# Queries and keys projected with tokens in the array and normed per token; GLA level scores for four heads at once

## The chip, the cores and the metric

The program runs on one core of one Trainium2 chip. A core has five engines that run at the same time, each with its own instruction queue in program order: TensorE (PE, the matrix array; PEld is its loading of the stationary operand), VectorE (DVE), ScalarE (ACT), GpSimd (POOL) and SyncE (SP, which here issues weight transfers). The metric is device time in microseconds (us), from one execution's start to its end; the median of three runs is used.

## The reference

The model is two blocks. The first has two layers, each over 256 tokens x and 256 context tokens z of width 1024: half a SwiGLU feed-forward, token mixing, half a SwiGLU. The second block (fox attention and retention) is not touched. The token mixing projects the normed tokens with `w_in` and mixes with four methods side by side:

```python
na_q = lambda p: rms_norm(heads(p['na_q'], 4, 64), na_q_norm)      # na_k, gqa_q, gqa_k likewise
b_x = neighborhood_attention(na_q(px), na_k(px), na_v(px), kz_na, vz_na, na_rpb)
c_x = gla_output(ox_gla, px['gla_r'], gla_norm)                    # gated linear attention, 4 heads of 32
qx_gqa = apply_rope(gqa_q(px), cos, sin)                           # rotated by position, x only
kx_gqa = apply_rope(gqa_k(px), cos, sin)
d_x = block_attention(qx_gqa, concat([kx_gqa, kz_gqa]), concat([gqa_v(px), vz_gqa]))
out_x = concat([a_x, b_x, c_x, d_x])                               # a_x: a Fourier mix
```

`rms_norm` here runs over the 64 channels of one head of one token: `x * rsqrt(mean(x*x) + eps) * gain`. In the last layer only x goes on, so z needs keys and values there but no queries. GLA's decayed scores are computed at several levels (block sizes 64, 128, 32, 16, ... of the token axis), and the results are merged under masks.

## The kernel before

All data are fp32. Big matmuls keep fp32 precision by splitting both operands in a rounded part `hi` and a rest `lo` and doing three matmuls (`mm3`, L615 to L619: hi*hi, H_lo*hi, H_hi*lo). Activations live transposed: `H` holds channels on the partitions and tokens along the free axis (x in columns 0 to 255, XR; z in 256 to 511, ZR). Weights stream in chunks of 512 KB through SP's queue; ACT makes `hi` (L593), DVE makes `lo` (L595); `take` and `drop` hand a chunk's pair to its user and free it. `make_plan` lists the chunks in the order in which they are used.

The order of instructions on every engine is made in Python by a list scheduler (`Sched`, L327 to L411): each piece of work is a generator that yields an engine and an estimated time, and the piece that can start earliest is put next. A piece that fills only part of the array (`pe_part`: the level scores and the attention scores) is spaced out by a factor 1.7 among the others. On the chip each engine then runs its list in order.

`mix1` (L1179) does the token mixing. Its main thread goes through the windows of `w_in`: a window is one projection of some 128 columns over all tokens, 8 steps of `mm3`. The values (GV) are projected with tokens as the stationary operand, so that they come out with tokens on the partitions; queries and keys (NQ, NK, QQ, QK) are projected with the weights as the stationary operand, so that they come out transposed: 64 channels of a head on partitions and tokens along the free axis. In that form the mean over a head's channels runs across partitions: `normed` (L1519) copies the projection out, squares it on ACT (L1526), and `head_rstd` (L658) sums squares by tiny matmuls (L664, two columns per token tile), takes the power on POOL (L641), spreads the result by a copy (L669) and transposes it back (L673); DVE multiplies it in (L1530). For GQA's x tokens a rotation follows: a matmul with a permutation (L1536), DVE times sin (L1539), POOL times cos (L1542), POOL add (L1544).

Beside the windows run: `level` (L1306), which makes the decayed q and k of one GLA level (POOL differences L1321, ACT exp, DVE product) and lets `score` (L1378) multiply two heads at once, in two groups of 32 rows of the array (L1389), twice per level; `merge` brings them under the masks. `pair` (L1554) does two heads of attention: `scores` (L1601), `soft` (L1605: DVE maximum L655 or L1611, ACT exp L1617, DVE reciprocal L1621, DVE scale L1623, PE transposes L1627), and the product with the values (L1573). Neighbourhood attention adds a bias of 128 KB per head, loaded through POOL's queue (L1591) into two tiles. After the windows follow Fourier, GLA's outputs, what is left of attention, and then `w_out`.

At the start of `mix1` the second token range's norm is still in work: POOL's queue holds the load of the small parameters `pp` (L1192), memsets, two bias loads, two gains (L1200) and then the power `r` (L641) of that norm, which PE transposes (L649) and DVE multiplies in (L843, L848) to finish `H`.

Of the kernel before, what the change touches and what calls it, by code (L numbers as in the profile page):

```python
# [38 lines left out]
                          np.arange(C_QV, C_QV + 128)]).reshape(2, 336)  # L39
WOUT_ROWS = np.concatenate([np.arange(768), 768 + QPERM])  # L40
# [31 lines left out]
def rot_matrix(half, n):  # L72
    p = np.zeros((2 * half, 2 * half))
    for i in range(half):
        p[i, i + half] = -1.0
        p[i + half, i] = 1.0
    return block_diag(p, n).T


def consts1():  # L80
# [6 lines left out]
    c.add("ropeP", rot_matrix(32, 2))  # L87
# [4 lines left out]
    ang = ang.astype(np.float64)[:, p % 32].T  # L92
    c.add("cos", np.cos(ang))
    c.add("sin", np.sin(ang))
# [53 lines left out]
def params1(inp):  # L148
    packs = []
    for l in range(DEPTH):  # L150
# [8 lines left out]
        c.add("wg", wg)  # L159
        packs.append(c)  # L160
# [3 lines left out]
def params2(inp):  # L164
    packs = []
    for l in range(DEPTH):
# [10 lines left out]
             bgf=(5, 6), bgb=(6, 7), wg=(7, 263))  # L177
# [52 lines left out]
def make_plan():  # L230
# [19 lines left out]

    for l in range(DEPTH):
        ffn(("ffn1_w1", "ffn1_w3", "ffn1_w2"), l)
        last = l == DEPTH - 1
        if last:
            w("w_in", l, 0, KD, cols(C_GQ))
            for t in range(2):
                w("w_in", l, 0, KD, cols(C_NQ, t))
        for half in range(2):
            for k0, n in ((0, 3), (3, 3), (6, 2)):
                w("w_in", l, k0, n, GV_COLS[half])  # L260
# [4 lines left out]
        for t in range(2):  # L265
            w("w_in", l, 0, KD, cols(C_NK, t))
            if not last:
                w("w_in", l, 0, KD, cols(C_NQ, t))
        w("w_in", l, 0, KD, cols(C_QK))
        for t in range(2):  # L270
            w("w_in", l, 0, KD, C_QQ + QPERM[128 * t:128 * t + 128])
# [159 lines left out]
def pet(k=1):  # L431
    return "PE", k * 0.06
# [22 lines left out]
class Net:  # L455
# [723 lines left out]
    def mix1(self, l, last, hwait):  # L1179
# [8 lines left out]
        p_sem, lev_sem, pair_sem = Sem(nP), Sem(2), Sem(nPT // 2)  # L1188
        ev = defaultdict(Ev)

        pp = mp.tile([128, 263], F32, name="pp")
# [114 lines left out]
        def level(s):  # L1306
# [42 lines left out]
            left = [2]  # L1349
            for h in (0, 2):  # L1350
                self.spawn(score(s, h, Q, K, left))
# [26 lines left out]
        def score(s, h0, Q, K, left):  # L1378

            bs = []  # L1380
            for h in range(2):
                b = yield from self.bank()
                bs.append(b[:, :T])
            yield pe_part(128, 4 * ns)
            for u in range(2 * ns):
                i = u ^ 1 if s == 128 else u
                for h in range(2):
                    r = 32 * (h0 + h)
                    PE.matmul(bs[h][:, 128 * u:128 * u + 128], K[r:r + 32, 128 * u:128 * u + 128],  # L1389
                              Q[r:r + 32, 128 * i:128 * i + 128], start=True, stop=True, tile_position=(r, 0))  # L1390
            left[0] -= 1
            if left[0] == 0:
                self.release(lev_sem)
            for h in range(2):
                self.spawn(merge(s, h0 + h, bs[h]))
# [832 lines left out]
```

## Time and profile before

| | before |
|---|---|
| median of 3 runs | 2482.75 us (2481.01 to 2484.56) |
| profiled execution | 2481.66 us, span 2479.9 us |
| mean granted TensorE clock | 0.996 |
| instructions | 38754 |
| busy PE / DVE / ACT / POOL | 98% / 64% / 39% / 20% of the span |

Busy shares are over the whole span; the token mixing of layer 0 lies at about 405 to 600 us and that of layer 1 at about 1400 to 1580 us. The times of the rows further down are counted from the span's start. A fp32 matmul shows as two records, hence twice the number of matmuls in the counts of L1389, L664 and L1536.

### The profile page before, as it was taken

To read this page: it belongs to the slowest core of one execution; us is meant where nothing else is said; L and a number is where in the kernel's file an instruction comes from. 1 tells how busy PE (TensorE), PEld (TensorE's weight loads), DVE (VectorE), ACT (ScalarE), POOL (GpSimd) and SP (SyncE) were. 2 spreads that over 40 slices of the span, in tenths; PEclk is the share of its full clock that TensorE was granted. 3 is DMA by queue.
4 is the path that set the end of the run, shared out by engine and by line. 5 is a ranking of instruction groups with operands and counts; after the bars stand their busy time and mean duration, and the time that the engine had idled before them with its cause. 6 is when DMAs were issued, how large, how long until landed. Compare 5 with 4: busy or idle time off the path is not lost.

```text
span 2479.9 us, 38754 instructions
## 1 busy us (share of the span) xinstructions
PE 2431.0 (98%) x15186; PEld 2120.1 (85%) x15186; DVE 1582.1 (64%) x2655; ACT 960.9 (39%) x1599; POOL 490.7 (20%) x492
## 2 busy tenths in 40 slices
PE   7999999999999999999999999999999999999998
PEld 5888888786888888888888887999988999988998
DVE  4878746566667676656652657766668655768654
ACT  4322224445432222332222345644535534445443
POOL 0201011331110101110101224100232422222322
PEclk9999999999999999999999999999999999999999
DMA  7665532210345553345642322555433654434652
GB/s 284 228 194 190 180 101 92 71 56 22 128 153 169 169 170 121 134 145 189 211 160 79 100 89 70 196 182 181 159 124 108 214 172 164 147 116 162 204 182 83
DMA packets 105735, 365.87 MB, mean 148 GB/s; under 512 B 13168, under 2 KB 15376, under 8 KB 105040
## 3 DMA queue, kind: packets, MB, share of 16 engines
q1 hardware_dynamic: 82768, 286.58, 35.1%
q10 hardware_dynamic: 21712, 72.98, 9.2%
q0 software_dynamic: 1072, 3.82, 0.5%
q8 instruction: 120, 1.97, 0.3%
q14 instruction: 63, 0.52, 0.1%
HBM read 360.09 MB, written 1.05 MB: 146 GB/s over the span
## 4 chain that ended last, share of the span: by engine, by line
PE 89%; DVE 4%; issue 3%; POOL 2%; ACT 1%; DMA 1%; POOLq 0%; DVEq 0%; SPq 0%; ACTq 0%
PE bank L617 27%; PE bank L618 27%; PE bank L619 27%; DVE lo L595 1%; PE bank L1573 1%; PE bank L1601 1%; POOL lev L1321 1%; DMA raw<-in_dram 1%; PE bank L1627 1%; POOL r L641 1%; ACT hi L593 1%; PE bank L1389 1%; PE bank L2027 0%; PE bank L2072 0%; PE bank L2008 0%
## 5 line engine op out<-in xcount | busy, mean ns | idle before, releaser
L617 PE MATMUL bank<-H_hi,hi 128*128 128x512 f32 (+3 forms) x3000 | 998.9, 334 | 0.3 <-ACT H_hi L846 0.3
L618 PE MATMUL bank<-H_lo,hi 128*128 128x512 f32 (+3 forms) x3000 | 984.5, 329 | 1.9 <-DVE H_lo L848 1.9
L619 PE MATMUL bank<-H_hi,lo 128*128 128x512 f32 (+3 forms) x3000 | 983.0, 328 | 2.1 <-DVE lo L595 2.1
L593 ACT CAST hi<-raw 128x1024 fp32r<-128x1024 f32 (+3 forms) x538 | 543.5, 1023 | 1017.6 <-PE bank L618 901.0
L595 DVE TENSOR_TENSOR lo<-raw,hi 128x1024 fp32r<-128x1024 f32 (+3 forms) x538 | 657.5, 1232 | 353.7 <-ACT hi L593 349.5
L617 PEld LDWEIGHTS bank<-H_hi,hi 128*128 128x128 f32 x3000 | 566.0, 189 | 60.5 <-issue 7.5
L619 PEld LDWEIGHTS bank<-H_hi,lo 128*128 128x128 f32 x3000 | 567.1, 189 | 53.2 <-DVE lo L595 2.5
L618 PEld LDWEIGHTS bank<-H_lo,hi 128*128 128x128 f32 x3000 | 567.6, 189 | 51.1 <-DVE H_lo L848 2.5
L617 PE MATMUL bank<-gh,hi 128*128 128x512 f32 (+2 forms) x1119 | 369.4, 330 | 1.1 <-ACT gh L925 1.1
L618 PE MATMUL bank<-gl,hi 128*128 128x512 f32 (+2 forms) x1119 | 369.0, 330 | 0.6 <-POOL gl L927 0.6
L619 PE MATMUL bank<-gh,lo 128*128 128x512 f32 (+2 forms) x1119 | 368.8, 330 | 0.0
L927 POOL TENSOR_TENSOR gl<-f,gh 128x512 fp32r<-128x512 f32 (+2 forms) x136 | 170.2, 1252 | 969.5 <-ACT gh L925 962.9
L720 DVE CUSTOM_DVE_ANT_0 prod<-mraw,crow 128x1024 f32<-128x1024 f32 x224 | 307.3, 1372 | 2.9
L617 PEld LDWEIGHTS bank<-gh,hi 128*128 128x128 f32 x1119 | 211.0, 189 | 22.5 <-ACT gh L925 1.5
L618 PEld LDWEIGHTS bank<-gl,hi 128*128 128x128 f32 x1119 | 211.1, 189 | 22.1 <-POOL gl L927 1.2
L619 PEld LDWEIGHTS bank<-gh,lo 128*128 128x128 f32 x1119 | 211.0, 189 | 20.7
L1025 DVE SCALAR_TENSOR_TENSOR X<-bank,mod,X 128x256 f32<-128x256 f32 x192 | 87.0, 480 | 137.2 <-PE bank L619 137.1
L925 ACT CAST gh<-f 128x512 fp32r<-128x512 f32 (+2 forms) x136 | 68.6, 506 | 141.0 <-DVE f L917 108.5
L910 POOL TENSOR_TENSOR s<-s,rstd 128x272 f32<-128x272 f32 (+1 forms) x44 | 66.9, 1521 | 184.8 <-ACT s L908 184.7
L641 POOL TENSOR_TENSOR r<-v,half 128x2 f32<-128x2 f32 (+3 forms) x43 | 48.1, 1120 | 193.1 <-DVE v L637 192.8
L917 DVE TENSOR_TENSOR f<-s,bank 128x512 f32<-128x512 f32 (+2 forms) x114 | 64.2, 564 | 34.5 <-POOL s L910 28.6
L804 POOL TENSOR_TENSOR acc<-acc,sq 128x256 f32<-128x256 f32 (+1 forms) x33 | 42.2, 1278 | 170.7 <-ACT sq L801 170.7
(279 smaller groups left out, 2017.1 us busy)
## 6 DMA issues: line engine op xcount, KB each, us to landing
raw<-in_dram SPq DMA_DIRECT2D x422, 512.0 KB, 3.4
mraw<-in_dram ACTq DMA_DIRECT2D x128, 512.0 KB, 4.3
raw<-in_dram SPq DMA_DIRECT2D x96, 448.0 KB, 3.3
mraw<-in_dram SPq DMA_DIRECT2D x16, 512.0 KB, 4.1
raw<-in_dram SPq DMA_DIRECT2D x8, 504.0 KB, 3.2
crow<-in_dram ACTq DMA_DIRECT2D x3, 1024.0 KB, 5.2
raw<-in_dram SPq DMA_DIRECT2D x8, 384.0 KB, 4.9
X<-in_dram SPq DMA_DIRECT2D x4, 512.0 KB, 8.1
```

What stands on the lines that cost most here:

```text
L593: self.ACT.copy(hi, raw)
L595: self.DVE.tensor_tensor(lo, raw, hi.bitcast(F32), op=ALU.subtract)
L617: self.PE.matmul(ps, a[0], b[0], start=first, stop=False)
L618: self.PE.matmul(ps, a[0], b[1], start=False, stop=False)
L619: self.PE.matmul(ps, a[1], b[0], start=False, stop=last)
L641: self.POOL.tensor_tensor(r[:, :n], v[:, :n], self.half[:, :n], op=ALU.pow)
L720: i = self.DVE.tensor_tensor_reduce(prod, got[c], rows[:, s], 1.0, 0.0, ALU.mult, ALU.add, m[:, s, k:k + 1])
L910: self.POOL.tensor_tensor(s, s, late[1], op=ALU.mult)
L917: self.DVE.tensor_tensor(f, s, pb[:, :w], op=ALU.mult)
L925: self.ACT.copy(hi, f)
L927: self.POOL.tensor_tensor(lo, f, hi.bitcast(F32), op=ALU.subtract)
L1025: self.DVE.scalar_tensor_tensor(o, ps[:, r[0] - r0:r[1] - r0], self.mods[l][i][:, s, m:m + 1], o, ALU.mult, ALU.add)
```

## The change

Normed queries and keys are projected like the values: tokens stationary, 256 or 384 columns (NK and QK in one) streaming, in passes of two token tiles (z tiles 2 and 3 first, then 0 and 1). They come out with tokens on the partitions, so that a head's mean runs along the free axis: ACT squares, DVE reduces per head and scales, POOL takes the power, DVE multiplies from the bank. GQA's x tokens are rotated by four DVE operations with tables that POOL makes at the start of `mix1` from cos, sin and the gains. Then PE transposes 128 x 128 blocks, and ACT copies them out with the gain. A pair of attention now waits for all token tiles of its queries and keys. `score` takes four banks and multiplies four heads in four groups of 32 rows; it is no longer spaced out as partial work.

```diff
-        def score(s, h0, Q, K, left):
+        def score(s, Q, K):
+            yield four_sem
             bs = []
-            for h in range(2):
+            for h in range(4):
                 b = yield from self.bank()
                 bs.append(b[:, :T])
-            yield pe_part(128, 4 * ns)
+            self.release(four_sem)
+            yield *pe32(128, 2 * ns), Sched.LAT
             for u in range(2 * ns):
                 i = u ^ 1 if s == 128 else u
-                for h in range(2):
-                    r = 32 * (h0 + h)
+                for h in range(4):
+                    r = 32 * h
                     PE.matmul(bs[h][:, 128 * u:128 * u + 128], K[r:r + 32, 128 * u:128 * u + 128],
                               Q[r:r + 32, 128 * i:128 * i + 128], start=True, stop=True, tile_position=(r, 0))
...
+        rope = mp.tile([128, 2, 2, 2, 64], F32, name="rope")
+        rows = mp.tile([128, 2, 64], F32, name="rows")
+        g = par("gqa_rows").rearrange("p (i c) -> p i c", i=2)
+        POOL.tensor_scalar(rows[:, 0], g[:, 0], 0.125, None, ALU.mult)
+        POOL.tensor_copy(rows[:, 1], g[:, 1])
+        for i in range(2):
+            for tt in range(2):
+                cs, sn = (self.c1(x)[:, 64 * tt:64 * tt + 64] for x in ("cos", "sin"))
+                POOL.tensor_tensor(rope[:, i, 0, tt], cs, rows[:, i], op=ALU.mult)
+                for a, b in ((0, 32), (32, 0)):
+                    POOL.tensor_tensor(rope[:, i, 1, tt, a:a + 32], sn[:, a:a + 32], rows[:, i, b:b + 32], op=ALU.mult)
+        def normed(tt, ps, parts):
...
+            ACT.activation(y, ps, AF.Square)
...
+            DVE.tensor_reduce(v, split(y), AX.X, ALU.add)
+            DVE.tensor_scalar(v, v, 1 / 64, EPS, ALU.mult, ALU.add)
...
+            POOL.tensor_tensor(rr, v, self.half[:, :nh], op=ALU.pow)
+            DVE.tensor_tensor(split(y), split(ps), rr.unsqueeze(2).to_broadcast([128, nh, 64]), op=ALU.mult)
...
+            for name, c, w, gain, i in parts:
+                if i is None or tt >= 2:
+                    continue
...
+            for j in range(0, n, 128):
+                PE.transpose(tp[:, j:j + 128], y[:, j:j + 128], self.ident)
...
-            rb = yield from self.head_rstd(sq, n)
...
-                PE.matmul(b[:, :256], self.c1("ropeP"), dst[:, :256], start=True, stop=True)
...
+            yield from self.wait_all([ev[q, 2 * s], ev[q, 2 * s + 1]] + [ev[k, t] for t in keys]
+                                     + [ev["v", h, t] for h in range(2) for t in keys])
...
+            yield from heads("nq", [(0, 1)])
...
+        yield from heads("k", [(2, 3), (0, 1)])
+        if not last:
+            yield from heads("nq", [(2, 3), (0, 1)])
```

Line numbers after the change are one lower up to `score` and higher behind it: L1389 is L1388, L641 is L640, L1601 is L1636, L1627 is L1662.

On POOL at the head of layer 1's mixing, before (a name left of the arrow is written, right of it read; `r` is the rstd of the second token range):

```order
103 L1591 DMA bias_10501<-in_dram 128x256
104 L1200 TENSOR_SCALAR gain_10478<-pp 128x1 x2
105 L641 TENSOR_TENSOR r<-v,half 128x2
106 L641 TENSOR_TENSOR r<-v,half 128x4 x2
107 L1321 TENSOR_TENSOR lev<-Fc 128x2x64 x2
```

and after:

```order
111 L1199 TENSOR_SCALAR gain_10635<-pp 128x1 x2
112 L1519 TENSOR_SCALAR rows<-pp 128x64
113 L1520 COPY rows<-pp 128x64
114 L1524 TENSOR_TENSOR rope<-k_mix,rows 128x64
115 L1526 TENSOR_TENSOR rope<-k_mix,rows 128x32 x2
116 L1524 TENSOR_TENSOR rope<-k_mix,rows 128x64
117 L1526 TENSOR_TENSOR rope<-k_mix,rows 128x32 x2
118 L1524 TENSOR_TENSOR rope<-k_mix,rows 128x64
119 L1526 TENSOR_TENSOR rope<-k_mix,rows 128x32 x2
120 L1524 TENSOR_TENSOR rope<-k_mix,rows 128x64
121 L1526 TENSOR_TENSOR rope<-k_mix,rows 128x32 x2
122 L640 TENSOR_TENSOR r<-v,half 128x2
```

Fourteen operations (`rows`, `rope`) now stand between the gains and `r`; the same rows stand at the head of layer 0.

On PE in layer 1's windows, before (L1389 the level scores, L664 and L673 the sums and the transposes of `head_rstd`, L1601 scores of neighbourhood attention, the rest projection):

```order
6461 L1389 MATMUL bank<-lev 128x128 x4
6462 L664 MATMUL bank<-k_mix,p_10484 128x2 x4
6463 L617 MATMUL bank<-H_hi,hi_64 128x512
6464 L618 MATMUL bank<-H_lo,hi_64 128x512
6465 L619 MATMUL bank<-H_hi,lo_65 128x512
6466 L1389 MATMUL bank<-lev 128x128 x4
6467 L617 MATMUL bank<-H_hi,hi_64 128x512
6468 L618 MATMUL bank<-H_lo,hi_64 128x512
6469 L619 MATMUL bank<-H_hi,lo_65 128x512
6470 L1601 MATMUL bank<-nk_10505,nq_10506 128x512 x2
6471 L673 MATMUL bank<-k_89,p_10484 128x128 x4
6472 L617 MATMUL bank<-H_hi,hi_64 128x512
```

and after (L1388 the level scores of four heads, the rest the projection with tokens in the array):

```order
6557 L618 MATMUL bank<-hi_68,H_lo 128x384
6558 L1388 MATMUL bank<-lev 128x128 x8
6559 L616 MATMUL bank<-hi_68,H_hi 128x384
6560 L617 MATMUL bank<-lo_69,H_hi 128x384
6561 L618 MATMUL bank<-hi_68,H_lo 128x384
6562 L1388 MATMUL bank<-lev 128x128 x8
6563 L616 MATMUL bank<-hi_70,H_hi 128x384
```

Groups of four matmuls have become groups of eight, and there are half as many; the sums (L664) are gone.

On PE at the end of layer 1's last window, after (L1636 the scores, L1568 the transposes of normed queries, L1662 the transposes of the softmax):

```order
6766 L617 MATMUL bank<-H_lo,hi_64 128x256
6767 L618 MATMUL bank<-H_hi,lo_65 128x256
6768 L1636 MATMUL bank<-nk,nq 128x512 x2
6769 L1568 MATMUL bank<-k_89,p_10640 128x128 x2
6770 L1434 MATMUL bank<-k_89,lev 128x128 x4
6771 L1568 MATMUL bank<-k_89,p_10641 128x128 x2
6772 L1444 MATMUL bank<-vt_10650,p_10640 128x256
6773 L1444 MATMUL bank<-vt_10651,p_10640 128x256
6774 L1662 MATMUL bank<-k_89,p_10639 128x128 x4
```

The scores of nk and nq, of which one stands among the projections in the PE rows of before (L1601), now begin behind the last projection.

## Rows read from the trace of the kernel before

**Rows 1.** Busy share of each engine, from the page

```profile
PE 2431.0 (98%) x15186; PEld 2120.1 (85%) x15186; DVE 1582.1 (64%) x2655; ACT 960.9 (39%) x1599; POOL 490.7 (20%) x492
```

**Rows 2.** Windows: from:to, length, busy us of each engine, clock, DMA

```profile
455.90:561.00 105.10, 101.94 (x627) 80.73 (x626) 66.11 (x112) 42.33 (x75) 40.20 (x47) 0.97 0.22 71
...
1530.00:1580.00 50.00, 48.11 (x373) 40.40 (x372) 34.87 (x72) 30.66 (x65) 11.58 (x12) 1.00 0.37 126
```

**Rows 3.** Timeline of PE, layer 0: start, us, line, records

```profile
461.09 0.39 PE L618 MATMUL bank<-H_lo,hi 128*128 128x512 f32 x1
...
461.32 0.39 PE L619 MATMUL bank<-H_hi,lo 128*128 128x512 f32 x1
...
461.64 1.16 PE L1389 MATMUL bank<-lev 32*128 32x128 f32 x16
...
463.07 0.40 PE L618 MATMUL bank<-H_lo,hi 128*128 128x512 f32 x1
```

**Rows 4.** Timeline of PE, layer 1, the same place

```profile
1478.75 0.40 PE L619 MATMUL bank<-H_hi,lo 128*128 128x512 f32 x1
...
1479.08 0.71 PE L1389 MATMUL bank<-lev 32*128 32x128 f32 x8
...
1480.06 0.40 PE L618 MATMUL bank<-H_lo,hi 128*128 128x512 f32 x1
```

**Rows 5.** PE's instructions by line and shape: records, busy us, mean ns

```profile
L664 PE MATMUL bank<-k_mix,p 128*128 128x2 f32 x108 | 13.8, 248 | 0.4 <-ACT p L1526 0.4
...
L1536 PE MATMUL bank<-qq,k_mix 128*128 128x256 f32 x8 | 2.4, 378 | 0.0
```

**Rows 6.** Timeline of PE at a group of L664, layer 0

```profile
465.40 1.05 PE L664 MATMUL bank<-k_mix,p 128*128 128x2 f32 x8
...
466.31 0.48 PE L617 MATMUL bank<-H_hi,hi 128*128 128x512 f32 x1
```

**Rows 7.** Timeline of PE, a projection of 256 columns

```profile
398.02 0.28 PE L619 MATMUL bank<-gh,lo 128*128 128x256 f32 x1
...
398.14 0.28 PE L617 MATMUL bank<-gh,hi 128*128 128x256 f32 x1
```

**Rows 8.** PE's waits in 408 to 640; timeline; window 480 to 500

```profile
PE bank L1627 <- DVE p L1623: 2.8, 4, 1.1
...
PE bank L673 <- DVE p L669: 0.8, 1, 0.8
...
498.10 0.63 PE L618 MATMUL bank<-H_lo,hi 128*128 128x512 f32 x1
...
498.53 0.63 PE L619 MATMUL bank<-H_hi,lo 128*128 128x512 f32 x1
...
480.00:500.00 20.00, 17.07 (x108) 11.64 (x110) 15.48 (x33) 8.44 (x16) 8.16 (x12) 0.91 0.17 53
```

**Rows 9.** Timeline of POOL, heads of layer 0 and layer 1

```profile
412.64 0.42 POOL L1200 TENSOR_SCALAR gain<-pp 128x1 f32<-128x1 f32 x2 [1.45 <-DMA pp<-in_dram]
...
413.04 0.97 POOL L641 TENSOR_TENSOR r<-v,half 128x2 f32<-128x2 f32 x1
...
1407.09 1.25 POOL L1200 TENSOR_SCALAR gain<-pp 128x1 f32<-128x1 f32 x2 [0.74 <-DMA pp<-in_dram]
...
1409.32 1.00 POOL L641 TENSOR_TENSOR r<-v,half 128x2 f32<-128x2 f32 x1 [0.98 <-DVE v L637]
```

**Rows 10.** DVE by line in 1500 to 1640; timeline of PE; POOL's line; DMA issues

```profile
L655 DVE CUSTOM_DVE_ANT_0 bank<-bank,bias 128x512 f32<-128x512 f32 x2 | 1.4, 696 | 0.0
...
L1623 DVE TENSOR_SCALAR p<-p,rs 128x512 f32<-128x512 f32 x6 | 3.1, 512 | 0.1
...
492.02 1.13 PE L1601 MATMUL bank<-nk,nq 64*128 64x512 f32 x4
...
L1591 POOL DMA_DIRECT2D bias<-in_dram x16 | 9.0, 566 | 19.1 <-DVE m L655 15.1 <-DVE m L656 3.4 <-DVE rs L1621 0.4
...
bias<-in_dram POOLq DMA_DIRECT2D x8, 128.0 KB, 2.5
```

More of the change, by code (lines that the diff above doesn't have):

```diff
@@ L91, in consts1 @@
                           (t % 64).astype(np.float32)[:, None] * inv], axis=1).astype(np.float32)
-    ang = ang.astype(np.float64)[:, p % 32].T
+    ang = ang.astype(np.float64)[:, np.arange(64) % 32].reshape(2, 128, 64).transpose(1, 0, 2)
     c.add("cos", np.cos(ang))
-    c.add("sin", np.sin(ang))
+    c.add("sin", np.where(np.arange(64) < 32, -1, 1) * np.sin(ang))
     a64 = 2 * np.pi * np.outer(np.arange(64), np.arange(64)) / 64
@@ L159, in params1 @@
         c.add("wg", wg)
+        c.add("gqa_rows", np.broadcast_to(np.concatenate([np.asarray(inp[n][l]) for n in ("gqa_q_norm", "gqa_k_norm")]),
+                                          (128, 128)))
         packs.append(c)
@@ L249, in ffn, with tok @@
                 w(names[2], l, k0, k1 - k0, cols(0, m))
+    def tok(l, name):
+        c, n = TOK[name]
+        for k in range(0, KD, n):
+            w("w_in", l, k, min(n, KD - k), c)
     for l in range(DEPTH):
@@ L255, in make_plan @@
             w("w_in", l, 0, KD, cols(C_GQ))
-            for t in range(2):
-                w("w_in", l, 0, KD, cols(C_NQ, t))
+            tok(l, "nq")
         for half in range(2):
-            for k0, n in ((0, 3), (3, 3), (6, 2)):
-                w("w_in", l, k0, n, GV_COLS[half])
+            tok(l, half)
             if half == 0:
@@ L264, in make_plan @@
                     w("w_in", l, 0, KD, cols(C_GQ))
[L265 to L271, printed above, removed]
+        tok(l, "k")
+        if not last:
+            tok(l, "nq")
+        tok(l, "qq")
         for t in range(2):
@@ L1348, in level @@
                 return
-            left = [2]
-            for h in (0, 2):
-                self.spawn(score(s, h, Q, K, left))
+            self.spawn(score(s, Q, K))
         def few(s, prods):
@@ L1552, in mix1, with pair @@
             POOL.memset(t[:, 256:], 0.0)
-        def pair(kt, s, q, k, keys, vcol, bias):
-            yield from self.wait_all([ev[q], ev[k]] + [ev["v", h, t] for h in range(2) for t in keys])
+        def pair(kt, s, q, qi, k, ki, keys, vcol, bias):
+            yield from self.wait_all([ev[q, 2 * s], ev[q, 2 * s + 1]] + [ev[k, t] for t in keys]
+                                     + [ev["v", h, t] for h in range(2) for t in keys])
             yield pair_sem
@@ L1564, in pair @@
                 sub += evs
-                self.spawn(scores(s, qn[q], qn[k], keys, qt, pT, bias, evs))
+                self.spawn(scores(s, qn[q][:, qi], qn[k][:, ki], keys, qt, pT, bias, evs))
             yield from self.wait_all(sub + [win_done])
@@ new lines, in mix1, with heads @@
+        NORMED = {"k": (("nk", 0, 256, par("na_k_norm"), None), ("qk", 256, 128, par("gqa_k_norm"), 1)),
+                  "nq": (("nq", 0, 256, gain8[:, 0:1], None),), "qq": (("qq", 0, 256, gain8[:, 1:2], 0),)}
+        def heads(name, passes):
+            yield from tok(name, passes, lambda t, ps: normed(t, ps, NORMED[name]))
+        if last:
+            w = yield from self.take("w_in", l, 0, KD, cols(C_GQ))
+            b = yield from self.bank()
+            yield from self.gemm([(b[:, :256], w)], self.H, *XR, lambda k: hwait(k, *XR))
+            self.drop()
+            gla_q(b[:, :256])
+            yield from heads("nq", [(0, 1)])
```

161 lines of the change are left out of this document (76 added, 85 removed).

## The prediction

> **What bounds the kernel now.** I read the page's busy shares first: TensorE (PE) is busy 98% of the span, VectorE (DVE) 64% [rows 1]. So a change pays by the PE time it removes, and costs where it makes PE wait. The windows by stage then show where that holds. The mixing stage of layer 0 has PE busy 101.94 of 105.10 us and DVE 66.11; before layer 1's w_out (1530 to 1580) PE has 48.11 of 50 and DVE 34.87 [rows 2]. The list of PE's instructions by line gives the sizes of what is removed, the timelines what each group costs between its neighbours, the waits what PE waits for. The sum is made against the profiled execution, 2481.66 us; the median of the runs is 1.09 us above it, and I add that at the end.
>
> **Level scores: fewer groups on PE.** A level's scores stand as a small group between projection matmuls. In layer 0 one group (8 matmuls, 16 records) pushes the next matmuls apart: from 461.32 to 463.07 there are 1.75 us, of which two steps of the projection's cadence (461.09 to 461.32, 0.23) are work that stands there anyway: 1.28 us per group [rows 3]. In layer 1 (half as many matmuls) it is 1480.06 - 1478.75 - 0.47 = 0.84 us [rows 4]. The four more matmuls cost 1.16 - 0.71 = 0.45 us [rows 3, 4], so 0.4 us of each group is entry and exit. After the change six groups of twice the matmuls stand in each layer where there were twelve. If four heads run at once, a new group lasts as long as an old one: 6 x 1.28 + 6 x 0.84 = 12.7 us saved. If only two run at once, as now, just twelve entries go: 12 x 0.4 = 4.8 us. I take 12.7, because the two heads of a group already run beside each other, and keep 4.8 as the end of the range. The Trainium skill, "TensorEngine Tiling (Array Packing)", Key Properties, says that different tiles of the array can load and multiply in parallel, which would give the 12.7, and that a change of tiling mode drains the engine, which agrees with the 0.4 us.
>
> **The rest that PE loses and gains.** The tiny matmuls of L664 (sums of squares per head): from the buffers `p` 108 records, 54 matmuls, 13.8 us busy [rows 5]; 48 of them, those of queries and keys, go: 12.3 us busy. In place, 1.05 us busy push the next matmul by 0.91 [rows 6], so 12.3 x 0.87 = 10.6 us. The rotation matmul L1536 lasts 0.6 us (two records of 378 ns [rows 5] that overlap a little); six go, 6 x 0.6 x 0.87 = 3.1 us. Transposes stay 28 and 20 in number, but in 20 groups instead of 14: at half a group's entry each, 6 x 0.2 = 1.2 us more. Projections: with tokens in the array, a matmul streams 256 or 384 columns instead of 512; 256 columns stand 0.12 apart [rows 7], two of them as long as one of 512, and 384 lies between, so the total changes by 0.4 us at most; I put +0.4. PE's own work: -12.7 - 10.6 - 3.1 + 1.2 + 0.4 = -24.8 us.
>
> **Waits in the windows of layer 0.** Now PE waits there four times, 2.8 us, on L1623 (the softmax scale) before the transposes L1627, and twice 0.8 us on the copy L669 before L673 [rows 8]. After two of these waits the 512-column matmuls stand 0.43 apart (498.10 to 498.53) instead of 0.23 [rows 8]: the granted clock of that stretch is 0.91 [rows 8], so its lower level (1.2 GHz) for about eight matmuls, 1.6 us. The order shows the neighbourhood softmaxes (nk, nq) behind the windows afterwards and L669 gone: -2.8 - 1.6 - 1.6 = -6.0. The new chain ACT square, DVE reduce, POOL power, DVE scale, PE transpose has a whole projection pass as cover; I put +1.5 for its misses. Net -4.5.
>
> **The two heads: fourteen POOL instructions in front of a rstd.** GpSimd (POOL) runs in order, and in each layer its queue gets 14 small operations (the rope tables) behind the two gains and in front of the `r` (L641) of the second token range, for which PE's L649 waits in the order. In layer 0 POOL is done with the gains at 413.06 and `r` starts at once (413.04), so every us of the tables lands on PE. The trace has no 128x64 or 128x32 operation: the two gains (one column) took 0.42 us together in layer 0 and 1.25 in layer 1 [rows 9], 0.21 to 0.63 each. So 14 cost 2.9 to 8.8 us; I take the geometric middle, 0.36 each, 5.0 us. Layer 0: +5.0, and after such an idle stretch the lower clock once more, +1.6. Layer 1: POOL is free at 1407.09 + 1.25 = 1408.34, with tables at 1413.3 instead of 1409.32: +4.0. There GLA's query is now alone in step with the arriving H tiles and the normed query follows: by the order 34 instead of 15 matmuls of 256 columns are left behind the last tile, 19 x 0.12 = 2.3, half of it covered by waits: +1.2. Heads: +11.8. What queues behind `r`: DVE's multiplications L843 of that range, and with them the H tiles and the weight splits.
> The Trainium skill, "SBUF - State Buffer", section "SBUF: two separate sides", says that a DVE operation with two SBUF operands and a GpSimd operation that reads SBUF exclude each other for their whole length; by it the tables take the longer time, which is a rival below.
>
> **The tails: attention moved behind the windows.** The order has all scores of nk and nq at the end of the last window (layer 1: all four there; layer 0: the eight of 512 keys), since a pair now waits for all token tiles. The work of PE is the same there; that of DVE meets a stretch in which PE has few projections left: by the order 21 matmuls of w_out stand before the last transpose. A softmax of 512 costs DVE at least 0.70 + 0.51 us [rows 10], eight of them 9.7 us in each layer, until now spread over windows where DVE had 39 us free [rows 2]. Bounds per layer: 0 (all beside PE's other work) to 9.7. I take 6.5 in layer 1 and 3 in layer 0, where the z tokens' attention still stands in the windows: +9.5.
>
> **Sum.** -24.8 - 4.5 + 11.8 + 9.5 = -8.0: 2473.7 us, and 2474.8 beside the median.
>
> **Rivals.**
> (A) Nothing comes back. The tails cost 0, the tables their lower bound (layer 0 +2.9, layer 1 1408.34 + 2.9 = 1411.2, +1.9), no new waits: -24.8 - 6.0 + 4.8 = -26.0, 2456.7. For it: DVE is free 36% of the span. Against: POOL works in order, and in layer 0 `r` starts the moment the gains end [rows 9].
> (B) Slower: the neighbourhood softmaxes become a chain. There are two bias tiles; the next pair's two loads start only when the pair before has taken its maximum. One round: scores 1.13, maxima 2 x 0.70, two issues of 0.57, landing 2.5 [rows 10]: 6.2 us, four rounds 24.8 per layer, in the windows hidden, behind them not. If other work covers 9.7 of it, the tails lose 30.2 instead of 9.5: +12.7, 2495. It is slower from tails of 22.5 us together. Against: PE has GLA, fourier and GQA work to put between.
> (C) The tables take 0.63 each, 8.8 us (gains of layer 1): heads 8.8 + 1.6 + 7.8 + 1.2 = 19.4 instead of 11.8, -0.4: 2482.4.
> (D) Only two heads run at once: 7.9 us less saved, -0.1: 2482.7; the change doesn't do what it says.
>
> **Chances.** Forecast 0.42 (own range 2467 to 2481), A 0.18, B 0.14, C 0.14, D 0.12. What a measurement here can tell from no change is about 0.2%, 5 us. Faster (below 2477.8): most of the forecast's case, 0.35, A 0.18, a quarter of C and D 0.07: 0.60. Slower: B 0.13, C and D together 0.05: 0.18. Same: 0.22. Range 2457 (A) to 2491 (most of B).
>
> **What would show it.** Score groups with four heads: as long as 1.16 and 0.71 us if they run together, about 2.0 and 1.2 if not. L664 left with the twelve matmuls of GLA's output alone. POOL between gain and `r`: 14 operations of 0.36 us, and PE's wait for `r` of some 5 and 4 us. PE busy share of the last 50 us before w_out: lower than 48.11 of 50; if it is as high, the tails cost nothing. Layer 0's windows: no waits for L1623. The forecast is wrong if the tables run in under 3 or over 8 us, or if the tails lose over 20.

## The result and the profile after

The changed kernel takes 2503.7 us (median of 4 runs, 2500.2 to 2504.6) against 2481.9 for the kernel before beside it: ratio 1.0086, interval 1.0068 to 1.0103, some 22 us slower. The forecast was 2474.8, range 2457 to 2491. Its profiled execution took 2503.83 us, span 2502.1, with a mean granted TensorE clock of 0.987 (0.996 before).

The page's busy shares, which answer to [rows 1]:

```profile
PE 2423.0 (97%) x15222; PEld 2127.3 (85%) x15222; DVE 1592.3 (64%) x2706; ACT 960.9 (38%) x1616; POOL 493.8 (20%) x514
```

PE is busy 8 us less, and the span is 22 us longer: PE waits more. Where, the windows by stage tell. Four stages hold the whole difference: the head of each layer's mixing (from the end of the feed-forward to the end of the GK window) and the rest up to the end of w_out. Columns: from:to, length, busy us of PE, PEld, DVE, ACT and POOL, granted clock, DMA share, GB/s. Before:

```profile
408.61:438.62 30.01, 29.16 (x159) 24.77 (x158) 20.23 (x42) 13.12 (x27) 3.95 (x10) 1.00 0.30 95
...
438.62:642.62 204.00, 199.06 (x1208) 151.45 (x1208) 123.71 (x253) 97.90 (x201) 59.61 (x71) 0.97 0.18 59
...
1403.77:1438.17 34.40, 32.15 (x213) 30.11 (x212) 24.11 (x50) 15.31 (x32) 6.83 (x12) 1.00 0.38 123
...
1438.17:1572.04 133.87, 131.23 (x927) 107.30 (x926) 92.99 (x190) 72.46 (x143) 42.85 (x63) 1.00 0.27 88
```

After:

```profile
407.50:444.49 36.99, 32.00 (x161) 26.52 (x160) 21.69 (x44) 15.09 (x29) 7.66 (x24) 0.95 0.22 69
...
444.49:648.31 203.82, 187.85 (x1264) 151.77 (x1264) 130.97 (x283) 96.44 (x212) 57.54 (x70) 0.94 0.18 61
...
1409.41:1450.18 40.77, 34.52 (x207) 32.14 (x206) 24.66 (x51) 16.68 (x33) 10.53 (x26) 0.87 0.30 96
...
1450.18:1592.88 142.70, 131.44 (x909) 111.68 (x909) 94.81 (x209) 70.81 (x145) 39.67 (x58) 0.93 0.25 84
```

Length less PE busy is idle time. The granted clock stands at 1.00 or at 0.50 in these traces. The stretches at 0.50 within the four stages (three before, nine after) add up to these rows, before and after:

```profile
sum 10.24, PE 9.89 PEld 7.06 DVE 8.01 ACT 6.63 POOL 5.96; mean PE 3.30 PEld 2.35 DVE 2.67 ACT 2.21 POOL 1.99
...
sum 58.03, PE 47.70 PEld 41.67 DVE 40.60 ACT 17.37 POOL 24.68; mean PE 5.30 PEld 4.63 DVE 4.51 ACT 1.93 POOL 2.74
```

Half of the time that PE is busy at 0.50 is lost to the lower clock (one less the clock, times a stage's whole length, would count time in which PE stood still a second time). What is left is PE's work at full speed. Summed over the four stages:

| us | before | after | difference |
|---|---|---|---|
| length | 402.3 | 424.3 | +22.0 |
| PE idle | 10.7 | 38.5 | +27.8 |
| lost to the lower clock | 4.9 | 23.8 | +18.9 |
| work at full speed | 386.7 | 362.0 | -24.7 |

The work on PE fell by 24.7 us, where 24.8 were forecast; 27.8 us of new idle time and 18.9 us of lower clock took it back and 22 more. By stage the heads are 7.0 and 6.4 us longer, layer 0's rest is unchanged (-0.2), layer 1's rest 8.8 longer.

Each rest has two parts: the windows, up to the end of the last projection of `w_in`, and the tail behind it, with the remaining attention and `w_out`. The two tails (layer 0, layer 1) before:

```profile
560.87:642.62 81.75, 79.97 (x481) 54.75 (x480) 48.20 (x131) 46.74 (x118) 13.57 (x16) 0.98 0.14 49
...
1518.44:1572.04 53.60, 52.61 (x398) 42.93 (x397) 39.30 (x79) 30.88 (x66) 12.27 (x13) 1.00 0.29 96
```

and after:

```profile
561.47:648.31 86.84, 80.71 (x489) 55.26 (x488) 52.58 (x139) 48.47 (x118) 15.82 (x20) 0.98 0.16 52
...
1520.50:1592.88 72.38, 65.91 (x447) 51.10 (x445) 49.34 (x121) 40.83 (x92) 11.03 (x14) 0.91 0.25 80
```

The heads. POOL's timeline, the first table operation and `r` (here L640), layer 0 and layer 1, answers to [rows 9]:

```profile
412.56 0.38 POOL L1519 TENSOR_SCALAR rows<-pp 128x64 f32<-128x64 f32 x1
...
416.32 0.72 POOL L640 TENSOR_TENSOR r<-v,half 128x2 f32<-128x2 f32 x1
...
1414.15 0.39 POOL L1519 TENSOR_SCALAR rows<-pp 128x64 f32<-128x64 f32 x1
...
1418.32 0.73 POOL L640 TENSOR_TENSOR r<-v,half 128x2 f32<-128x2 f32 x1
```

The 14 tables took 416.32 - 412.56 = 3.8 us and 1418.32 - 1414.15 = 4.2 us, 0.27 and 0.30 each on average. Single operations differ by what DVE does beside them, as layer 1 shows:

```profile
1414.88 1.02 DVE L847 SCALAR_TENSOR_TENSOR H_lo<-mt,mod,H_hi 128x256 fp32r<-128x256 f32 x2
1415.83 0.86 DVE L842 SCALAR_TENSOR_TENSOR mt<-X,mod,bank 128x256 f32<-128x256 f32 x2
...
1415.58 0.50 POOL L1524 TENSOR_TENSOR rope<-k_mix,rows 128x64 f32<-128x64 f32 x1
...
1416.46 0.31 POOL L1524 TENSOR_TENSOR rope<-k_mix,rows 128x64 f32<-128x64 f32 x1
```

Beside L847, which reads two operands from SBUF, the operation takes 0.50 us; beside L842, one of whose operands comes from a bank, 0.31. PE, behind `r`:

```profile
417.09 0.43 PE L648 MATMUL bank<-k,r 128*128 128x128 f32 x2 [4.59 <-POOL r L640]
...
418.28 0.48 PE L617 MATMUL bank<-lo,H_hi 128*128 128x336 f32 x1
...
418.56 0.48 PE L618 MATMUL bank<-hi,H_lo 128*128 128x336 f32 x1
...
421.37 0.32 PE L617 MATMUL bank<-lo,H_hi 128*128 128x336 f32 x1
...
421.52 0.31 PE L618 MATMUL bank<-hi,H_lo 128*128 128x336 f32 x1
```

PE waited 4.59 us and then ran its 336-column matmuls 0.28 apart, its lower level (1.2 GHz), until 421; then 0.15 apart. In layer 1's head the clock fell at 1414.3, behind three waits for tiles of H (0.62, 0.81 and 0.98 us) and before the wait of 3.62 us for `r`, and stayed low until 1424.6.

The score groups. PE in layer 0's windows, answers to [rows 3]:

```profile
480.33 1.17 PE L1388 MATMUL bank<-lev 32*128 32x128 f32 x32
...
488.00 0.89 PE L1388 MATMUL bank<-lev 32*128 32x128 f32 x4 [6.02 <-DVE p L1548]
...
489.51 2.71 PE L1388 MATMUL bank<-lev 32*128 32x128 f32 x28 [0.62 <-DVE p L1548]
...
493.17 0.41 PE L617 MATMUL bank<-lo,H_hi 128*128 128x256 f32 x1
...
493.38 0.41 PE L618 MATMUL bank<-hi,H_lo 128*128 128x256 f32 x1
```

A group of four heads (32 records) takes 1.17 us: four at once, as forecast. But the next one stands 6.02 us with its first banks (the wait is for the multiplication `p` L1548 of the new norm), 0.62 again, and then group and projection run at the lower clock (256 columns 0.21 apart instead of the 0.12 of [rows 7]) until 496. What the norm waits for, in the same stretch on ACT, DVE and POOL:

```profile
480.10 2.92 ACT L592 CAST hi<-raw 128x1024 fp32r<-128x1024 f32 x3
...
482.93 0.86 ACT L1538 ACTIVATE p<-bank 128x384 f32<-128x384 f32 x2
```

```profile
481.37 3.49 DVE L594 TENSOR_TENSOR lo<-raw,hi 128x1024 fp32r<-128x1024 f32 x3
...
484.77 1.01 DVE L1541 TENSOR_REDUCE v<-p 128x6 f32<-128x384 f32 x2
...
487.30 0.56 DVE L1548 TENSOR_TENSOR p<-bank,r 128x384 f32<-128x384 f32 x1 [1.31 <-POOL r L1546]
...
488.90 0.55 DVE L1548 TENSOR_TENSOR p<-bank,r 128x384 f32<-128x384 f32 x1
```

```profile
485.94 2.61 POOL L1546 TENSOR_TENSOR r<-v,half 128x6 f32<-128x6 f32 x2 [6.84 <-DVE v L1543]
```

The projection ended at 480.1. Its squares (L1538) come after three weight casts at 482.93, the sums behind three weight rests at 484.77, the two powers from 485.94 to 488.55, the multiplications at 487.30 and 488.90: nine us from the projection's end to the release of its banks. PE's list has the next score group at this place and works in order. In layer 1's rest the longest waits are for the norm's rotation (L1563, 3.4 us in two), the softmax (L1656, 2.2 in one) and the merging of level scores (L1405, 2.1 in two).

### The profile page after: what moved, and what is told of

It is laid out like the page before. It is cut to its first block, busy times and chain, and to the rows that moved or that the text cites. A ratio compares the mean times of both kernels' runs of the same rounds, so it can differ in the third digit from the quotient of the medians.

```text
span 2502.1 us, 38905 instructions
## 1 busy us (share of the span) xinstructions
PE 2423.0 (97%) x15222; PEld 2127.3 (85%) x15222; DVE 1592.3 (64%) x2706; ACT 960.9 (38%) x1616; POOL 493.8 (20%) x514
## 4 chain that ended last, share of the span: by engine, by line
PE 87%; DVE 4%; issue 3%; POOL 3%; ACT 2%; DMA 1%; POOLq 0%; SPq 0%; DVEq 0%; ACTq 0%
PE bank L616 27%; PE bank L617 27%; PE bank L618 26%; DVE lo L594 1%; PE bank L1608 1%; POOL lev L1320 1%; PE bank L1636 1%; PE bank L1662 1%; POOL r L640 1%; PE bank L2059 0%; POOL r L1546 0%; PE bank L2104 0%; ACT hi L592 0%; PE bank L2040 0%; PE bank L2151 0%
## 5 line engine op out<-in xcount | busy, mean ns | idle before, releaser
L616 PE MATMUL bank<-H_hi,hi 128*128 128x512 f32 (+3 forms) x2888 | 954.2, 331 | 1.0 <-ACT H_hi L845 1.0
L617 PE MATMUL bank<-H_lo,hi 128*128 128x512 f32 (+3 forms) x2888 | 942.6, 327 | 2.1 <-DVE H_lo L847 2.1
L618 PE MATMUL bank<-H_hi,lo 128*128 128x512 f32 (+3 forms) x2888 | 941.5, 326 | 0.9 <-DVE lo L594 0.9
L616 PEld LDWEIGHTS bank<-H_hi,hi 128*128 128x128 f32 x2888 | 544.7, 189 | 56.7 <-issue 7.5
L617 PEld LDWEIGHTS bank<-H_lo,hi 128*128 128x128 f32 x2888 | 545.9, 189 | 48.5 <-DVE H_lo L847 2.7
L618 PEld LDWEIGHTS bank<-H_hi,lo 128*128 128x128 f32 x2888 | 545.6, 189 | 48.4 <-DVE lo L594 1.3
L616 PE MATMUL bank<-hi,H_hi 128*128 128x336 f32 (+2 forms) x288 | 95.7, 333 | 1.7 <-DVE p L1548 1.3
L617 PE MATMUL bank<-lo,H_hi 128*128 128x336 f32 (+2 forms) x288 | 93.1, 323 | 0.0
L618 PE MATMUL bank<-hi,H_lo 128*128 128x336 f32 (+2 forms) x288 | 92.1, 323 | 0.4 <-DVE H_lo L847 0.4
```

What stands on the lines that cost most here:

```text
L616: self.PE.matmul(ps, a[0], b[0], start=first, stop=False)
L617: self.PE.matmul(ps, a[0], b[1], start=False, stop=False)
L618: self.PE.matmul(ps, a[1], b[0], start=False, stop=last)
```

## The experiments

Theories. H: the tables in front of `r` cost what PE waits there. C: each idle stretch is paid again in lower clock. P: groups that need four banks at once and banks that the norm holds for long starve PE together. N: the norm's chain is late, whoever holds banks. D: DVE is too busy. B: neighbourhood attention's bias loads in turn (rival B). T: keys come too late. Ratios are to the kernel before, run on the same chip.

**late_tables**: the tables' emission moved into a thread that waits for the first value tile.

```diff
+        def tables():
+            yield ev["v", 0, 0]
...
+        self.spawn(tables())
```

> The changed kernel with the 14 rope-table operations issued on POOL behind the second range's rstd (after the first value tile is out), nothing else. Theory H (the tables stand in front of the rstd and every us lands on PE): the waits of 4.6 and 3.6 us for r go down to 0.5 and 0.6, and the stretches at the lower clock behind them (about 12 matmuls x 0.13 and 24 x 0.095 us) go: -4.1 - 1.6 - 3.0 - 2.3 = -11 us, 2492 to 2494. Rival: what follows is set by the weight splits and DVE, and the time is given back in the windows: 2500 to 2504.

2503.4, ratio 1.0091 (1.0077 to 1.0105). The order shows why: the layer that places the instructions had pulled the tables, which depend on nothing late, forward to where they stood. It is a repeat of the changed kernel, and tells nothing of H.

**score_two**: the old `score` (two heads, two banks, paced) in the changed kernel.

```diff
-            self.spawn(score(s, Q, K))
+            left = [2]
+            for h in (0, 2):
+                self.spawn(score(s, h, Q, K, left))
```

> The changed kernel with the level scores two heads at once as before (paced, two banks a group). Theory P (a group of four needs four of the eight banks at once while the norm holds others, so PE stands 6.6 us in layer 0 and 2.1 in layer 1, with the lower clock behind it): these go, about -12, and the twelve groups come back, +12.7: 2503 to 2506. Rival Q (the norm's late release of its bank stalls whatever comes next, whether it needs two or four): the waits stay under another name and the groups cost 12.7 more: 2513 to 2518.

2507.0, 1.0105 (1.0092 to 1.0119), just above the range of P. Layer 0's wait at the fifth group is gone, others (3.0 us before the norm's transposes, 4.0 in layer 1) took its place. The rests are 203.45 and 145.78 us long, of which PE idles 10.8 and 16.3. In layer 0's windows idle time and lower clock together fall from 17.8 to 9.8 us, and the twelve groups take it back with 7.6 us of work. In layer 1 nothing is won. P holds for layer 0's windows and does not explain layer 1.

**before_four**: the reverse, the new `score` in the kernel before.

```diff
-            for h in (0, 2):
-                self.spawn(score(s, h, Q, K, left))
+            self.spawn(score(s, Q, K))
```

> The kernel before with the level scores four heads at once, nothing else. If the gain of the groups is real and four banks are there when the norm releases its bank after one copy: 2481.9 - 12.7 = 2469, with groups of 1.16 and 0.71 us. If a group of four banks stalls PE by itself (theory P without the norm): waits at the score of several us and 2478 to 2488.

2479.9, 0.9997 (0.9988 to 1.0006): the time of the rival, without its waits of several us. The two rests, as above for the kernel before:

```profile
436.45:632.50 196.05, 192.31 (x1209) 146.73 (x1209) 124.59 (x250) 99.77 (x204) 60.55 (x71) 0.97 0.18 61
...
1428.25:1568.32 140.07, 129.73 (x927) 107.00 (x927) 94.09 (x192) 72.89 (x142) 42.81 (x63) 0.98 0.24 84
```

Layer 0 is 8.0 us shorter (7.7 were forecast for its groups), layer 1 is 6.2 us longer: its work falls by 4.3 us, but PE idles 10.3 instead of 2.6 us, and the lower clock takes 2.8. The waits are many and small (six between 0.9 and 1.4 us, on ACT and DVE). In layer 1 the queries, Fourier and gate windows run over 256 tokens instead of 512, so PE has less to put between the groups; that this is the reason was not tested.

**four_first**: four heads in layer 0 only.

```diff
+            if not last:
+                self.spawn(score(s, Q, K))
+                return
+            left = [2]
             for h in (0, 2):
-                self.spawn(score(s, h, Q, K, left))
+                self.spawn(score2(s, h, Q, K, left))
```

> The kernel before with the level scores four heads at once in layer 0 only, two at once in layer 1 as before. In before_four the stages of layer 0 were 8.6 us shorter than before and those of layer 1 6.2 us longer. If the two are separate: 2481 - 8.6 = 2472. Rival (the gain of layer 0 is given back after it, or the loss of layer 1 has its cause in layer 0's order): 2478 to 2482.

2474.0, 0.9971 (0.9960 to 0.9982): 0.3% less than the kernel before, small but clear of the interval. Layer 0's rest is 196.0 us long, as in before_four; layer 1's:

```profile
1428.70:1562.48 133.78, 131.15 (x926) 107.33 (x926) 92.96 (x190) 72.91 (x144) 42.86 (x63) 1.00 0.27 87
```

The two layers are separate: layer 0 keeps its gain, layer 1 is as before.

**tables_behind**: late_tables with the 14 instructions tied to the GK window and held in program order.

```diff
+            yield ev["gk"]
+            self.tc.keep_in_program_order(POOL.tensor_scalar(rows[:, 0], g[:, 0], 0.125, None, ALU.mult))
...
```

> The changed kernel with the 14 table operations now truly behind r on POOL in both layers (in the run late_tables they had been pulled forward again and stood where they were); the order on PE is the same. Theory H: PE's waits for r fall from 4.6 and 3.6 us to about 0.5, the lower clock behind them goes (12 x 0.13 and 24 x 0.095 us): the stages up to the end of the GK window shrink from 37.2 to 30.5 (layer 0) and from 40.9 to 35 (layer 1): -11 to -13, 2491 to 2493. Rival: given back later in the windows, 2499 to 2504.

2496.1, 1.0059 (1.0047 to 1.0072): 7.6 us back, against 11 to 13 expected.

```profile
407.86:439.17 31.31, 30.45 (x160) 25.00 (x160) 21.77 (x44) 15.12 (x29) 8.18 (x24) 1.00 0.26 81
...
439.17:643.16 203.99, 187.17 (x1264) 151.07 (x1264) 130.87 (x283) 96.35 (x212) 57.60 (x70) 0.95 0.18 61
...
1404.34:1441.83 37.49, 34.40 (x207) 32.01 (x206) 24.36 (x51) 16.70 (x33) 9.93 (x26) 0.91 0.33 105
...
1441.83:1584.46 142.63, 131.65 (x910) 112.32 (x909) 94.57 (x209) 70.97 (x145) 39.71 (x58) 0.93 0.25 84
```

The heads shrink by 5.7 and 3.3 us, nothing is given back later (the rests are the same to 0.2). H holds. In layer 1 3.1 us of the head's 6.4 remain, as much as the lower clock takes there: behind the waits for arriving tiles of H (0.63, 0.83 and 0.98 us) the clock stands at 0.50 from 1409.2 to 1416.0, with PE busy for 6.2 us of it. Before, such waits stood there too (0.51, 0.28 and 0.86) with more matmuls between them, and the clock stayed at 1.00. This fits the forecast's GLA query alone in step with the tiles (1.2 were forecast), but was not tested by itself.

**filled**: useless matmuls in three of PE's waits.

```diff
+        fill = self.fill.pop(0) if self.fill else 0
+        for i in range(fill):
+            self.PE.matmul(rb[:, :256], self.H[0][:, 0, :128], self.H[0][:, 0, :256], start=True, stop=True)
```

> The changed kernel with useless matmuls put where PE waits: 32 of 256 columns before each layer's transposes of r (3.8 us of work into waits of 4.6 and 3.6 us) and 24 of 512 columns before layer 0's fifth score group (5.6 us into 6.0). Theory C (an idle PE is what lowers its granted clock, and the slow matmuls behind a wait double its price): the matmuls behind these three waits run at full speed: -1.6 (layer 0 head), -2.3 (layer 1 head), -3 (scores): 2496 to 2498, and the mean granted clock rises by 0.003 from 0.987. Rival: the lower clock is not tied to the idle time (or the fill only adds work): 2503 to 2506, clock as before.

2504.4, 1.0092 (1.0078 to 1.0106), the time of the rival; the rows tell why. PE at layer 0's head:

```profile
413.26 3.88 PE L649 MATMUL bank<-H_hi 128*128 128x256 f32 x31
...
418.75 0.31 PE L618 MATMUL bank<-lo,H_hi 128*128 128x336 f32 x1
...
418.90 0.31 PE L619 MATMUL bank<-hi,H_lo 128*128 128x336 f32 x1
```

Here PE works through the wait, and behind it the matmuls stand 0.15 apart at once, where the changed kernel had 0.28: the heads are 1.8 and 1.6 us shorter (1.6 and 2.3 expected), the mean clock rises to 0.991. In layer 1's head the time at 0.50 falls from 10.2 to 3.4 us. So C is shown at the heads. The third fill failed: the bank it wrote to was itself one of those waited for, so its 24 matmuls ran behind the 6.0 us, partly at the lower clock (8.0 us), and added what the heads had won.

**early_bank**: ACT copies the projection out first and releases the bank; squares go through the still empty destination.

```diff
-            ACT.activation(y, ps, AF.Square)
+            ACT.copy(y, ps)
+            self.unbank()
...
-            DVE.tensor_tensor(split(y), split(ps), rr.unsqueeze(2).to_broadcast([128, nh, 64]), op=ALU.mult)
-            self.unbank()
+            DVE.tensor_tensor(split(y), split(y), rr.unsqueeze(2).to_broadcast([128, nh, 64]), op=ALU.mult)
```

> The changed kernel with the norm's projection copied out of its bank by ACT at once and the bank released; squares go through the (still empty) destination, the scale multiplies the copy. Theory of the banks (the norm holds its bank until DVE's multiplication, after ACT, DVE, POOL, DVE): the wait for DVE p of 6.6 us in layer 0 goes with the lower clock behind it, 2.1 in layer 1: 2490 to 2495. Rival (DVE is late anyway, and PE waits for it at the transposes or the tail instead): 2500 to 2505.

2508.8, 1.0112 (1.0098 to 1.0126). Layer 0's rest is 205.2 us long, not shorter but 1.4 us longer: the long wait becomes a row of shorter ones, the longest 2.6 us on DVE's merging copies, which release the banks of the score group before. The bank that the norm holds is not the cause alone. The run is no clean test of it: the copy adds 4.9 us of work on ACT and 2.8 on DVE in this stage.

**no_chain**: tables_behind with the norm between projection and transposes left out (ACT's copy instead of the squares, no sums, power, scale or rotation).

```diff
-            ACT.activation(y, ps, AF.Square)
+            ACT.copy(y, ps)
...
-            DVE.tensor_reduce(v, split(y), AX.X, ALU.add)
-            DVE.tensor_scalar(v, v, 1 / 64, EPS, ALU.mult, ALU.add)
-            POOL.tensor_tensor(rr, v, self.half[:, :nh], op=ALU.pow)
-            DVE.tensor_tensor(split(y), split(ps), rr.unsqueeze(2).to_broadcast([128, nh, 64]), op=ALU.mult)
...
```

> tables_behind with the per-token norm's chain left out (no mean of squares, no power, no scale, no rotation: ACT copies the projection out, PE transposes it, ACT copies it on); the order on PE is the same but for a few rows. If the chain ACT, DVE, DVE, POOL, DVE and the banks that it holds are what PE stands for: the wait of 6.6 us of layer 0's fifth score group, those of 2.1 and 3.4 us in layer 1 and the lower clock behind them go: 16 to 22 us less than tables_behind, 2475 to 2480. Rival (the level scores' merging and the softmaxes on DVE set the pace of these stretches): the waits change names, 0 to 8 us less, 2488 to 2496.

2479.5, 0.9987 (0.9978 to 0.9995): 16.6 us less than tables_behind.

```profile
439.71:633.05 193.34, 183.20 (x1264) 147.91 (x1264) 116.57 (x231) 96.46 (x212) 46.95 (x58) 0.97 0.19 64
...
1431.76:1565.21 133.45, 125.64 (x908) 107.11 (x909) 83.60 (x174) 70.42 (x145) 31.27 (x51) 0.95 0.28 89
```

The rests are 10.7 and 9.2 us shorter at nearly the same order on PE: idle time falls by 6.7 and 3.2 us, the lower clock by 3.6 and 4.5. In layer 0's windows idle time and lower clock fall from 17.9 to 7.6 us together, near the 6.6 of the kernel before; in its tail they stay at 7.7. The chain is the largest single cause. What of it counts, its length, its banks or its work, this run does not separate: it takes 14.3 and 11.0 us of work from DVE too. In layer 1 even this is only as fast as before (133.45 to 133.87): there 7.8 us of idle and 5.7 of clock remain, 8.2 of them in the tail, with the softmaxes behind the windows.

**light_lo**: tables_behind with eight of the weight rests a layer made for 64 columns instead of 1024 (what the others hold is left over from earlier chunks).

```diff
+        j = 64 if name == "w_in" and c[0] in (C_NK, C_NQ, C_QQ) else w
-        self.DVE.tensor_tensor(lo, raw, hi.bitcast(F32), op=ALU.subtract)
+        self.DVE.tensor_tensor(lo[:, :j], raw[:, :j], hi[:, :j].bitcast(F32), op=ALU.subtract)
```

> tables_behind with the weight rests lo of eight chunks in each layer (keys, neighbourhood queries, GQA queries) made for 64 of 1024 columns only, at the same place in DVE's order; the order on PE is the same. It takes 8 x 1.15 = 9 us of DVE's work out of each layer's stretch of norms. If DVE's load there is what PE waits for: gaps and lower clock fall by more than half, -10 to -18: 2478 to 2486. Rival (the chain's latency and the places of the waiting instructions in PE's order, with DVE free time about): -2 to -6, 2490 to 2494.

2495.0, 1.0053 (1.0041 to 1.0065).

```profile
439.33:644.74 205.41, 189.34 (x1265) 152.48 (x1265) 125.87 (x282) 96.39 (x212) 56.84 (x70) 0.93 0.18 60
...
1442.38:1584.54 142.16, 130.89 (x908) 111.02 (x909) 90.45 (x208) 70.83 (x145) 39.10 (x58) 0.93 0.25 84
```

DVE has 5.0 and 4.1 us less to do in these stages (131 and 94.6 in tables_behind), and they are no shorter. What PE waits for at layer 0's fifth group (here L1390; the first wait ends with the norm's multiplication and the weight rest behind it):

```profile
PE bank L1390 <- DVE lo L596: 4.7, 1, 4.7
...
PE bank L1390 <- DVE PD L1407: 2.4, 1, 2.4
```

The norm's banks come 1.3 us earlier than in the changed kernel, where the first wait is 6.0, and the time is given back to the merging copies of the scores before, which hold the other banks. D falls as far as this load goes; it is about a third of what no_chain takes from DVE.

**bias_four**: tables_behind with the bias of a pair loaded before its buffers are taken, and four tiles in layer 1.

```diff
+            if bias is not None:
+                for hh in range(2):
+                    yield bias_sem
+                    bts[hh] = bias_free.pop(0)
+                    nc.gpsimd.dma_start(bts[hh][:, :256], self.nbias[l, bias + hh, :, qt])
             yield two_sem
```

> tables_behind with four bias tiles instead of two in layer 1 and each pair's bias loaded before its buffers and banks are taken (in layer 0 two tiles, loaded earlier too). If rival B of the prediction holds (scores, maxima, bias load in turn, 6.2 us a round) the stretch from layer 1's GK window to w_out's end loses two rounds' load, 4 to 7 us with the clock: 2489 to 2492. Rival (other buffers or DVE pace the rounds): within 2.5 us of tables_behind, 2494 to 2498.

2489.0, 1.0032 (1.0020 to 1.0044): 7.1 us less. PE's first and last scores of nk and nq in layer 1, tables_behind:

```profile
1512.34 1.13 PE L1647 MATMUL bank<-nk,nq 64*128 64x512 f32 x4
...
1539.85 1.13 PE L1647 MATMUL bank<-nk,nq 64*128 64x512 f32 x4
```

and bias_four (the last two pairs in one row):

```profile
1506.80 1.13 PE L1649 MATMUL bank<-nk,nq 64*128 64x512 f32 x4
...
1517.82 1.99 PE L1649 MATMUL bank<-nk,nq 64*128 64x512 f32 x8
```

From the first score to the start of the last, 27.5 us become about 12, and layer 1's rest goes from 142.6 to 139.3, its clock from 0.93 to 0.98. Rival B's chain was there; it cost about 3 us in layer 1 and 2 in layer 0, not the 15 a layer of the rival.

**early_keys**: tables_behind with the keys (and layer 0's nq) projected before the second half of the values.

```diff
                 for s in levels:
                     self.spawn(level(s))
+                yield from heads("k", [(2, 3), (0, 1)])
+                if not last:
+                    yield from heads("nq", [(2, 3), (0, 1)])
...
```

> tables_behind, and the keys (and layer 0's neighbourhood queries) projected before the second half of the values instead of after it, so that 15 us more of windows stand behind them and the norms have that time. Theory T (the tail and the waits in the windows come from norms that finish too late, all at the end): against tables_behind the stage from the second half of the values to w_out's end loses 5 to 9 us in layer 1 and 5 in layer 0: 2479 to 2483 in all. Rival (scores of neighbourhood attention stay behind the windows for another reason, buffers or pacing; the bursts of norm and level scores meet elsewhere): within 3 us of tables_behind.

2494.0, 1.0048 (1.0035 to 1.0061), 2 us less than tables_behind, within the runs' scatter. In the profiled execution, which was 3.6 us above the median, layer 1's rest is 137.5 instead of 142.6 us long: 5.1 gained, as T would have it. Layer 0's is 211.4 instead of 204.0: 7.4 lost, with PE idle for 21.6 us, since the norms now meet the level scores earlier (argued, not tested).

**repaired**: tables_behind, bias_four and, in layer 1 alone, early_keys.

```diff
+                if last:
+                    yield from heads("k", [(2, 3), (0, 1)])
...
-        yield from heads("k", [(2, 3), (0, 1)])
         if not last:
+            yield from heads("k", [(2, 3), (0, 1)])
             yield from heads("nq", [(2, 3), (0, 1)])
```

> The changed kernel with three repairs at once: tables behind r (measured -8), bias loads ahead with four tiles in layer 1 (-7), and in layer 1 alone the keys projected before the second half of the values (-5 in layer 1's stage in early_keys). If the three prices add up: 2503.6 - 8 - 7 - 5 = 2483, no slower than the kernel before. Rival (bias loads and early keys shorten the same tail and do not add): 2487 to 2490.

2485.7, 1.0016 (1.0007 to 1.0025). Between the two: 18 of the 22 us are back, and the changed form is still no faster than the kernel before.

## Why the prediction was wrong

The forecast's terms stand against idle time and lower clock, read as above, of the same stretches. Its waits in layer 0's windows (-4.5) and its tails (+9.5, of which 3 in layer 0) are there separately:

| PE idle and lower clock, us | before | after | difference | forecast |
|---|---|---|---|---|
| heads | 3.1 | 16.2 | +13.1 | +11.8 |
| layer 0, windows | 6.6 | 17.8 | +11.2 | -4.5 |
| layer 0, tail | 3.3 | 7.6 | +4.3 | +3 |
| layer 1, windows | 1.7 | 8.2 | +6.5 | 0 |
| layer 1, tail | 1.0 | 12.5 | +11.5 | +6.5 |
| PE's work at full speed | 386.7 | 362.0 | -24.7 | -24.8 |

- PE's own work: right. 32 records of four heads take 1.17 us, and the kernel before gains 8.0 us by them in layer 0, where 7.7 were forecast. In layer 1 its work fell by 4.3 us (5.0 forecast), and waits turned that into a loss of 6.2 (before_four), which the forecast did not see.
- The heads: the mechanism was right, the size nearly. The tables took 3.8 and 4.2 us (5.0 taken); moving them gave 9.0 back in the heads' stages and 7.6 in the time. Rival C, the tables at 0.63 each, fell: they took 0.27 and 0.30 on average. The rule of the Trainium skill ("SBUF - State Buffer", "SBUF: two separate sides") that was held against the change is seen in these rows, at a lower price: 0.50 us instead of 0.31 beside DVE's L847, about 0.4 us of the tables in layer 0 and 0.8 in layer 1. In all eleven runs with these tables no 128x64 operation that met no such DVE operation took over 0.33 us; of the 36 that met one 13 took 0.50 to 0.53.
- The step that failed is "The new chain ... has a whole projection pass as cover; I put +1.5 for its misses", with the net -4.5 of layer 0's windows that hangs on it and nothing at all for layer 1's. Measured are +11.2 and +6.5. Without the chain (no_chain) layer 0's windows lose 10.3 us of idle time and lower clock, and the whole kernel takes 16.6 us less than tables_behind. By the rows of the stretch the chain is nine us long, since every link queues behind other work on its engine: casts on ACT, weight rests on DVE, two powers on POOL. The cover was counted in PE's rows as if PE could go on to something else; the next row of its list was a score group that needed four banks, or the transposes themselves.
- In layer 0's windows it takes both halves of the change. Idle time and lower clock there are 6.6 us with the old norm and groups of two (before), 5.5 with the old norm and groups of four (before_four), 9.8 with the new norm and groups of two (score_two), and 17.8 with both. The forecast priced the two apart.
- "L669 gone" (-1.6) was misread: one of the two waits of 0.8 us belongs to GLA's output norm, which stays. It lies in the tail, where PE now waits 3.2 and 1.1 us for that norm, most of layer 0's +4.3.
- The tails: +15.8 against +9.5, mis-sized. The window 1530 to 1580 that the prediction calls the stretch before layer 1's `w_out` holds `w_out` itself, from 1522 to 1572. Rival B had its chain right and its size far too large (bias_four: 3 and 2 us of stage time). early_keys shows 5.1 us in layer 1 for keys that come late.
- The clock runs through all of these. A new wait's clock was priced once, 1.6 us at layer 0's head; in the four stages it takes 18.9 us more than before, two thirds of what the new idle time takes. At the heads it is shown that the waits bring it (filled); for the waits in the windows it is read from the clock's records.
- Open: what of layer 1's loss comes from each of the norm's chain, the softmaxes behind the windows and the merging, and why four heads alone cost layer 1 of the kernel before 6.2 us in many small waits.

## What to carry to other kernels

On an engine that works in order, a shorter list is only worth its saving if the waits behind it are covered: follow the new dependency from engine to engine, count at each what is queued ahead of it, and compare the sum with what the waiting engine has to do before that row. Price a new wait of PE twice, once as idle time and once as slow matmuls behind it: here 27.8 us of the first brought 18.9 of the second. The share differs by place (score_two's layer 1 had 16.3 us idle and lost only 3.8 to the clock), so it is a price to check, not a rule. When two changes meet at one resource, as the norm and the groups of four did at the banks, price them together. And make such a choice per stage: four heads at once paid in layer 0 and cost in layer 1 of the same kernel.

## What was not expected of the hardware

After a wait of 4.6 us PE's 336-column matmuls stood 0.28 us apart, with the clock at 0.50 for 3.4 us, before they returned to 0.15, and did not when the same wait was filled with matmuls. In layer 1's head the lower clock came behind three waits of under 1 us each. Four matmuls of 32 rows each, in four row groups, ran as fast as two: 1.17 us for 32 records against 1.16 for 16. A GpSimd operation of 128x64 took 0.50 us instead of 0.31 beside a DVE operation with two SBUF operands.
